# Gate and up products of a transformer feed-forward stage in token-major blocks, with transposes into the down product

## Chip, core and metric

One core of a Trainium2 chip runs the whole program. The metric is the device time of one execution in microseconds (us), the median of several runs. TensorE does the matrix products, VectorE (DVE) and ScalarE (ACT) the elementwise work, GpSimd (POOL) a few reductions, SyncE (SP) issues the weight transfers.

## What is computed

Three transformer layers in a row on 256 tokens of 1024 channels, all in float32: two layers of a first kind and one of a second. Each ends in the same feed-forward stage, the part that the change touches:

```python
h = rms_norm(x, g_pre_ffn[l])
f = (jax.nn.silu(h @ w_gate[l]) * (h @ w_up[l])) @ w_down[l]    # 1024 -> 2816 -> 1024
x = x + rms_norm(f, g_post_ffn[l])
```

Ahead of it stand, by layer, attention with a short convolution and gates (the first two) or stick-breaking attention with a pooling mixer (the third); the third also takes scales and shifts from a small conditioning product (`w_cond_2`).

## The kernel before

**Exact products from rounded operands.** Every weight and every activation is split in two float32r parts: H, a rounded copy made on ACT (`nc.scalar.copy`, L267 for weights), and L, the remainder made on DVE (`tensor_sub`, L268). A product is three matmuls: H·H, H·L and L·H. So each weight tile of 1 MB (`raw`, [128, 2048]) costs two copies on ACT and two subtractions on DVE, one for each half.

**The weight stream.** All weights are packed on the host in the order of use (`ORDER`, from `stream_order` and `ffn_order`), one 1 MB transfer for each entry, issued on SP's queue. `get(key)` hands out the next entry and first issues transfers five entries ahead (`LOOK_RAW`, four `raw` buffers) and splits three entries ahead (`LOOK`). Halves of split weights live in nine buffers (`NSPLIT`). Entries named `cond` belong to the conditioning product: they aren't split, two DVE operations (L490) consume each. Nine of them lie in the feed-forward stage of layer 0 and nine in that of layer 1.

**Two forms of product.** `mmB` is channel-major: the weights are the stationary operand and the 256 tokens the moving one. One entry gives 256 output channels as [128 channels, 2 x 256 tokens] in one PSUM bank with 48 matmuls of 256 columns. `mmA4` is token-major: 128 tokens of the activation are stationary, 512 columns of weights move. Two entries (`h` = 0, 1) give 512 channels, for one token tile `t` at a time, with 24 matmuls of 512 columns into one PSUM bank; both token tiles take 48. The down product `mmD2` moves 512 columns of `w_down` and has the activation, channel-major, as stationary operand: 24 matmuls for an entry over two token tiles and two column halves.

**The feed-forward stage** (`ffn`, L496). The first 512 of the 2816 channels are token-major ("block A"): for each token tile gate (`pgA`), silu into `sA`, up (`puA`), `tensor_mul` on DVE (L520). Since down wants channels on the partitions, a task `ptf` then does four TensorE transposes (L505), the H copy (L508) and the L subtraction (L509) into `fA`. The other 2304 channels are nine channel-major blocks of 256 (`pg`, silu, `pu`, the DVE product L536, the split into `fHL` L539 and L540), already in the form that down wants. One down entry follows each of these blocks from the second on. The last four down entries form a tail (`row_out`), which goes token tile by token tile so that the norm behind it can begin.

**Order of the work.** The program is written out by hand with a planner: `pe(ns)` advances a clock by the planned TensorE time, `spawn(gen, delay)` books a task, and `tick()` between parts of products emits the tasks that have come due; `drain()` emits all that is left. A scheduler then fixes the order on each engine from priorities and its own timing, and may take a ready instruction ahead of one that it believes not ready. On the chip each engine works its list in order. Three pools matter here: eight PSUM banks (four of them the down accumulators `dn`), 17 large (`s4`) and seven small (`s2`) activation buffers.

Of the kernel before, what the change touches and what calls it, by code (L numbers as in the profile page):

```python
# [24 lines left out]
NKV = 4  # L25
HD = 64
DFF = 2816
NFB = (DFF - 512) // 256
NDOWN = DFF // 256
TAIL = 4  # L30
EPS = 1e-6
# [24 lines left out]


def ffn_order(l, cond):
    o = [("gA", l, 0), ("gA", l, 1), ("uA", l, 0), ("uA", l, 1)]
    nd = 0  # L60
    for i in range(NFB):
        o += [("g", l, i), ("u", l, i)]
        if i >= 1:
            o.append(("d", l, nd))
            nd += 1
        if cond:
            o.append(cond.pop(0))
    while nd < NDOWN:
        o.append(("d", l, nd))
        nd += 1  # L70
    assert not cond
    return o


# [42 lines left out]
def pack_weights(inp):  # L117
    splits = dict(q=0, kv=1024, cb=1536, cc=2560, cx=3584, ga=4608, gb=5632)
    out = np.empty((len(ORDER), P, CH), np.float32)

    def put(i, w, r0, nk, c0, nc_):
        src = w[r0:r0 + nk * P, c0:c0 + nc_]
        if nk == 4:
            out[i].reshape(P, nk, nc_)[...] = src.reshape(nk, P, nc_).transpose(1, 0, 2)
        else:
            out[i].reshape(P, 2, nk, nc_ // 2)[...] = src.reshape(nk, P, 2, nc_ // 2).transpose(1, 2, 0, 3)

    for i, k in enumerate(ORDER):
        n = k[0]
        if n == "q":  # L130
            put(i, inp["w_in"][k[1]], 512 * k[3], 4, 512 * k[2], 512)
        elif n == "kv":
            put(i, inp["w_in"][k[1]], 512 * k[2], 4, 1024, 512)
        elif n in ("cc", "cx", "cb", "ga", "gb"):
            put(i, inp["w_in"][k[1]], 0, 8, splits[n] + 256 * k[2], 256)
        elif n == "cp":
            put(i, inp["w_conv_proj"][k[1]], 0, 8, 256 * k[2], 256)
        elif n == "ap":
            put(i, inp["w_attn_proj"][k[1]], 0, 8, 256 * k[2], 256)
        elif n == "cond":  # L140
            put(i, inp["w_cond_2"][0], 256 * k[2], 2, 1024 * k[1], 1024)
        elif n in ("q2", "k2", "v2", "u2"):
            put(i, inp["w_in_2"][0], 512 * k[1], 4, 512 * ("q2", "k2", "v2", "u2").index(n), 512)
        else:
            l = k[1]
            sfx, li = ("", l) if l < 2 else ("_2", 0)
            if n == "wo":
                put(i, inp["w_out" + sfx][li], 256 * k[2], 2, 0, 1024)
            elif n == "d":
                put(i, inp["w_down" + sfx][li], 256 * k[2], 2, 0, 1024)  # L150
            elif n in ("gA", "uA"):
                w = inp[("w_gate" if n == "gA" else "w_up") + sfx][li]
                put(i, w, 512 * k[2], 4, 0, 512)
            else:
                w = inp[("w_gate" if n == "g" else "w_up") + sfx][li]
                put(i, w, 0, 8, 512 + 256 * k[2], 256)
    return out


# [1 line left out]
def tile_model(ctx: ExitStack, tc: tile.TileContext, x_in, wpack, sink, convw, gains, c_in,  # L161
# [9 lines left out]
    def s4(name, shape=(P, D), dt=F32):  # L171
        return ac.tile(list(shape), dt, tag="s4", name=name, bufs=NS4)
# [4 lines left out]
    def ps1(name, shape=(P, 512), dt=F32):  # L177
        return pp.tile(list(shape), dt, tag="B", name=name, bufs=8)
# [2 lines left out]
        return sm.tile([P, n], dt, tag="sm", name=name, bufs=24)  # L181

    class Pair:
        """A [128, 8, 256] operand as float32r pairs, in two tiles of four k-tiles each."""

        def __init__(self, name):
            self.name = name
# [15 lines left out]
            nc.scalar.copy(h, src)  # L203
            nc.vector.tensor_sub(self.ks(1, k0, n)[:, :, ts_], src, h.bitcast(F32))

# [1 line left out]
    clock = [0.0]  # L207
    tasks = []

# [27 lines left out]
    def mm(o, a, b, start, stop, **kw):  # L237
        nc.tensor.matmul(o, a, b, start=start, stop=stop, **kw)  # L238

# [1 line left out]
    state = dict(raw=0, spl=0, use=0)  # L241
    raws, HL = {}, {}

# [37 lines left out]
        state["use"] += 1  # L281
        return HL.pop(i)

# [1 line left out]
    HC = [slice(0, 512), slice(512, 1024)]  # L285
    xt = [cst.tile([P, D], F32, tag=f"x{t}", name=f"x{t}") for t in range(2)]

# [35 lines left out]
        nc.sync.dma_start(csb, c_in)  # L323
        nc.sync.dma_start(pscale, pool_scale)

# [1 line left out]
    def hp():  # L327
        return nullcontext() if state["use"] == 0 else tc.high_priority(offset=PRIO)

# [12 lines left out]
        return rs  # L342

    class Norm:
        """rms norm of a token tile: vec() the vector part, tr() the transposes into xp."""

        def __init__(self, t, G, S, xp, name):
            self.t, self.G, self.S, self.xp, self.name = t, G, S, xp, name
# [19 lines left out]
        def tr(self):  # L368
            ts_ = slice(self.t * P, (self.t + 1) * P)
            for j in range(2):  # L370
                pt = ps1(f"pt_{self.name}{j}", (P, 4, P))
                for k in range(4):
                    nc.tensor.transpose(pt[:, k, :], self.h[:, (4 * j + k) * P:(4 * j + k + 1) * P], ident)
                    pe(107)
                with hp():
                    self.xp.put(4 * j, 4, pt, ts_)
                if j == 0:
                    yield TR_GAP
            yield None

    class Post:
        """x += rms(acc) * G, half by half as the accumulator's banks complete."""

        def __init__(self, t, acc, G, name):
            self.t, self.acc, self.G, self.name = t, acc, G, name
# [16 lines left out]
                    if after is not None:  # L402
                        after(c)

# [1 line left out]
    def mmB(ps, w, xp):  # L406
        for c in range(2):
            o = ps[:, c * T:(c + 1) * T]
# [41 lines left out]
        tick()  # L450

    def row_out(chunks, accs, started, make_post, after):
        """chunks: [(w, fh, fl)]; per token tile, half by half, then the norms."""
        n = len(chunks)
        for t in range(2):
            post = make_post(t, accs[t])
            for c in range(2):
                for i, (w, fh, fl) in enumerate(chunks):
                    mmD2(accs[t], w, fh, fl, t, c, not started and i == 0, i == n - 1)
                post.half(c)  # L460
            after(t, post)
# [32 lines left out]
            nc.scalar.dma_start(modd[r:r + 1, :], mrow[0:1, :])  # L494

    def ffn(l, xp, norms, make_post, after):  # L496
        order = [k for k in ORDER if k[0] in ("g", "u", "d") and k[1] == l]
        gw = [get(("gA", l, h)) for h in range(2)]
        uw = [get(("uA", l, h)) for h in range(2)]
        fA = [s4(f"fA{j}{l}", (P, 4, T), F32R) for j in range(2)]  # L500

        def ptf(t, s):
            pt = ps1(f"ptf{l}{t}", (P, 4, P))
            for k in range(4):
                nc.tensor.transpose(pt[:, k, :], s[:, k * P:(k + 1) * P], ident)  # L505
                pe(107)
            dst = (slice(None), slice(None), slice(t * P, (t + 1) * P))
            nc.scalar.copy(fA[0][dst], pt)  # L508
            nc.vector.tensor_sub(fA[1][dst], pt, fA[0][dst].bitcast(F32))  # L509
            yield None  # L510

        for t in range(2):
            finish(norms[t].gen)
            pg = ps1(f"pgA{l}{t}")
            mmA4(pg, gw, xp, t)
            s = s2(f"sA{l}{t}")
            nc.scalar.activation(s, pg, AF.Silu)
            pu = ps1(f"puA{l}{t}")
            mmA4(pu, uw, xp, t)
            nc.vector.tensor_mul(s, pu, s)  # L520
            spawn(ptf(t, s), 2.0)
        fs = [(fA[0][:, 0:2], fA[1][:, 0:2]), (fA[0][:, 2:4], fA[1][:, 2:4])]
        tail = []
        accs = []
        for key in order:
            cond_due()
            if key[0] == "g":
                pg = ps1(f"pg{l}{key[2]}")
                mmB(pg, get(key), xp)
                s = s2(f"s{l}{key[2]}")  # L530
                last = nc.scalar.activation(s, pg, AF.Silu)
            elif key[0] == "u":
                pu = ps1(f"pu{l}{key[2]}")
                mmB(pu, get(key), xp)
                f = s2(f"f{l}{key[2]}")
                nc.vector.tensor_mul(f, pu, s)  # L536
                fHL = s4(f"fHL{l}{key[2]}", (P, 2, 2, T), F32R)
                fv = f.rearrange("p (k t) -> p k t", k=2)
                nc.scalar.copy(fHL[:, 0], fv)  # L539
                nc.vector.tensor_sub(fHL[:, 1], fv, fHL[:, 0].bitcast(F32))  # L540
                fs.append((fHL[:, 0], fHL[:, 1]))
            else:
                j = key[2]
                if not accs:
                    drain()
                    accs = [[ps1(f"dn{l}_{t}{c}") for c in range(2)] for t in range(2)]
                if j < NDOWN - TAIL:
                    w = get(key)
                    for t in range(2):
                        for c in range(2):  # L550
                            mmD2(accs[t], w, fs[j][0], fs[j][1], t, c, j == 0, False)
                else:
                    tail.append((get(key), fs[j][0], fs[j][1]))
        if l == DEPTH - 1:
            with tc.issue_after(last.ins):
                nc.scalar.preload_act_table_set("natural_log_exp_and_others")
        row_out(tail, accs, True, make_post, after)

# [1 line left out]
    def attention(l, q, kf, v, op):  # L560
        kTh = s4(f"kTh{l}", (P, NKV, T), F32R)
        kTl = s4(f"kTl{l}", (P, NKV, T), F32R)
# [177 lines left out]
            mp.put(2 * j, 2, a)  # L740
        return mp

# [1 line left out]
    def stick(hp, qT, kT, v2, mp, psz, pend):  # L744
        ws = [None, None]

# [102 lines left out]
                pass  # L849
        return mp  # L850

# [1 line left out]
    xp = Pair("x0")  # L853
    norms = [Norm(t, G0, None, xp, f"n0{t}") for t in range(2)]
    norms[0].vec()
# [164 lines left out]
```

## Time and profile before

| | |
|---|---|
| device time, 3 runs | 1199.77 us median (1198.21 to 1200.64) |
| span of the profiled execution | 1197.6 us |
| mean granted TensorE clock | 0.993 |
| TensorE matmul busy | 1164.8 us (97%) |
| DVE, ACT busy | 774.7 us (65%), 617.2 us (52%) |
| moved by DMA | 235.60 MB, mean 197 GB/s |

The profile covers one execution and gives its span from the first instruction to the last; it shows no time for what lies outside, so that execution's whole time isn't known. The median of the runs stands 2.2 us above the span. Busy matmul time counts each matmul to its modelled end, and neighbours overlap: the pace of a product is read from the distance of starts, which the chain of work that ended last gives as a duration and a count. Starts and durations are in us, means of one instruction in ns.

### The profile page before, as it was taken

The numbers are of one execution on the slowest core, as the hardware profiler recorded it, in microseconds if no ns is written. First come the engines' busy times: TensorE is split into PE (matmuls) and PEld (weight loads), VectorE is DVE, ScalarE is ACT, GpSimd is POOL, SyncE is SP. The second block draws the span as 40 slices with busy tenths as digits, with TensorE's granted clock in tenths as the row PEclk, the third lists the DMA queues.
The fourth block names the chain that finished last, engine by engine and source line by source line (L and its number), as shares of the span: only waits on it lengthen the run. The fifth ranks groups of instructions, "written<-read, shape, count | busy, mean of one in ns | idle before, by whom it ended". The sixth has DMA issues, their size and how long they took to land.

```text
span 1197.6 us, 19239 instructions
## 1 busy us (share of the span) xinstructions
PE 1164.8 (97%) x7880; PEld 1066.8 (89%) x7880; DVE 774.7 (65%) x958; ACT 617.2 (52%) x927; POOL 129.1 (11%) x146
## 2 busy tenths in 40 slices
PE   6999999999999999999999999999999999999997
PEld 5899899988999987998999978999987777999996
DVE  6767645769676747677757568675858448654542
ACT  5766555546444436656545455444445545544441
POOL 1021300010202001022220012020201002000000
PEclk9999999999999999999999999999999999999999
DMA  8733344646676665633357546584866345644520
GB/s 319 269 141 111 129 149 176 250 173 252 229 259 245 221 236 182 241 106 141 141 176 281 192 160 246 213 309 173 325 216 218 135 159 176 246 175 177 204 79 36
DMA packets 36256, 235.60 MB, mean 197 GB/s; under 512 B 4668, under 2 KB 5180, under 8 KB 9416
## 3 DMA queue, kind: packets, MB, share of 16 engines
q1 hardware_dynamic: 33696, 225.41, 51.9%
q10 hardware_dynamic: 2472, 8.96, 2.3%
q8 instruction: 62, 1.02, 0.3%
q14 instruction: 26, 0.21, 0.1%
HBM read 233.28 MB, written 1.07 MB: 196 GB/s over the span
## 4 chain that ended last, share of the span: by engine, by line
PE 51%; POOL 2%; ACT 1%; DVE 1%; issue 1%; POOLq 0%; DVEq 0%; ACTq 0%
PE pu L238 10%; PE dn L238 9%; PE pg L238 8%; PE wo L238 2%; PE pcp L238 2%; PE pap L238 2%; PE pga L238 2%; PE pgb L238 2%; PE pcx L238 2%; PE pcb L238 1%; PE pgA L238 1%; PE puA L238 1%; PE z L238 1%; PE po L238 1%; PE pv L238 1%
## 5 line engine op out<-in xcount | busy, mean ns | idle before, releaser
L268 DVE TENSOR_TENSOR L<-raw,H 128x1024 fp32r<-128x1024 f32 x374 | 472.6, 1270 | 228.3 <-ACT H L267 215.6
L267 ACT CAST H<-raw 128x1024 fp32r<-128x1024 f32 x374 | 390.7, 1049 | 366.8 <-PE pu L238 72.8
L238 PE MATMUL dn<-H,fHL 128*128 128x512 f32 x432 | 116.3, 391 | 0.0
L238 PEld LDWEIGHTS dn<-H,fHL 128*128 128x128 f32 x432 | 79.8, 188 | 15.6
L635 POOL TENSOR_SCALAR P<-P,rd 128x256 f32<-128x256 f32 x64 | 48.1, 769 | 228.2 <-DVE rd L633 67.3
L238 PE MATMUL dn<-L,fHL 128*128 128x512 f32 x216 | 66.8, 390 | 0.0
L493 POOL PARTITION_ALL_REDUCE mrow<-cacc x6 | 40.1, 6676 | 219.5 <-DMA raw<-in_wpack_dram 180.8
L490 DVE SCALAR_TENSOR_TENSOR cacc<-raw,silu_c,cacc 128x1024 f32<-128x1024 f32 x48 | 61.4, 1279 | 0.4
L238 PEld LDWEIGHTS dn<-L,fHL 128*128 128x128 f32 x216 | 40.6, 188 | 8.5
L536 DVE TENSOR_TENSOR f<-pu,s 128x512 f32<-128x512 f32 x27 | 18.6, 690 | 30.4 <-PE pu L238 30.4
L238 PE MATMUL pg<-xf1H,H 128*128 128x256 f32 x144 | 35.4, 283 | 0.0
L238 PE MATMUL pg<-xf0H,H 128*128 128x256 f32 x144 | 35.3, 283 | 0.0
L238 PE MATMUL pg<-xf2H,H 128*128 128x256 f32 x144 | 35.3, 283 | 0.0
L238 PE MATMUL pu<-xf0H,H 128*128 128x256 f32 x144 | 35.3, 283 | 0.0
L238 PE MATMUL pu<-xf0L,H 128*128 128x256 f32 x144 | 35.3, 283 | 0.0
L238 PE MATMUL pu<-xf1H,H 128*128 128x256 f32 x144 | 35.3, 283 | 0.0
L238 PE MATMUL pu<-xf1L,H 128*128 128x256 f32 x144 | 35.3, 283 | 0.0
L238 PE MATMUL pu<-xf2H,H 128*128 128x256 f32 x144 | 35.3, 283 | 0.0
L238 PE MATMUL pu<-xf2L,H 128*128 128x256 f32 x144 | 35.3, 283 | 0.0
L238 PE MATMUL pg<-xf1L,H 128*128 128x256 f32 x144 | 35.3, 283 | 0.0
L238 PE MATMUL pg<-xf0L,H 128*128 128x256 f32 x144 | 35.3, 283 | 0.0
L238 PE MATMUL pg<-xf2L,H 128*128 128x256 f32 x144 | 35.3, 283 | 0.0
(400 smaller groups left out, 3057.0 us busy)
## 6 DMA issues: line engine op xcount, KB each, us to landing
raw<-in_wpack_dram SPq DMA_DIRECT2D x209, 1024.0 KB, 4.9
raw<-in_wpack_dram SPq DMA_DIRECT2D x4, 512.0 KB, 8.5
gpm<-in_gains_dram ACTq DMA_DIRECT2D x3, 512.0 KB, 3.7
gpf<-in_gains_dram ACTq DMA_DIRECT2D x3, 512.0 KB, 5.1
gqf<-in_gains_dram ACTq DMA_DIRECT2D x2, 512.0 KB
out_dram<-x SPq DMA_DIRECT2D x4, 256.0 KB, 3.8
pmat<-in_pmat_dram SPq DMA_DIRECT2D x2, 384.0 KB, 6.8
x<-in_x_dram SPq DMA_DIRECT2D x2, 256.0 KB, 2.7
```

The lines of the kernel that those rows point to most:

```text
L238: nc.tensor.matmul(o, a, b, start=start, stop=stop, **kw)
L267: nc.scalar.copy(H, rv)
L268: nc.vector.tensor_sub(L, rv, H.bitcast(F32))
L490: nc.vector.scalar_tensor_tensor(a3, w[:, k], silu_c[:, 2 * j + k:2 * j + k + 1], a3, ALU.mult, ALU.add)
L493: nc.gpsimd.partition_all_reduce(mrow, a, P, bass_isa.ReduceOp.add)
L536: nc.vector.tensor_mul(f, pu, s)
L635: nc.gpsimd.tensor_scalar(Pt[:, hh, :], Pt[:, hh, :], rd[:, hh:hh + 1], 0.0, ALU.mult, ALU.add)
```

## The change

Gate and up take 512 channels at a time in token-major form five times (2560 channels); the last 256 channels stay channel-major. In each later token-major block gate runs for both token tiles first, then up for both. Each block ends in two `ptf` tasks, ten for a layer. In `ORDER` two down entries follow a token-major block from the second on (one after the last), and the `cond` entries lie after a block's gate and after its up entries, what is left ahead of the last 256 channels. `drain()` stays ahead of the first down product, which now comes right behind the second block's up. Comments that the diff drops are left out here.

```diff
-NFB = (DFF - 512) // 256
+NFB = DFF // 512
+REST = DFF - 512 * NFB
...
 def ffn_order(l, cond):
-    o = [("gA", l, 0), ("gA", l, 1), ("uA", l, 0), ("uA", l, 1)]
+    o = [(n, l, 0, h) for n in ("gA", "uA") for h in range(2)]
     nd = 0
-    for i in range(NFB):
-        o += [("g", l, i), ("u", l, i)]
-        if i >= 1:
+    for b in range(1, NFB):
+        for n in ("gA", "uA"):
+            o += [(n, l, b, h) for h in range(2)] + cond[:1]
+            del cond[:1]
+        while nd < min(2 * b, NDOWN - TAIL):
             o.append(("d", l, nd))
             nd += 1
-        if cond:
-            o.append(cond.pop(0))
+    o += cond
+    cond.clear()
+    o += [("g", l), ("u", l)]
     while nd < NDOWN:
...
+        def gate(b, t, w):
+            pg = ps1(f"pgA{l}{b}{t}")
+            mmA4(pg, w, xp, t)
+            s = s2(f"sA{l}{b}{t}")
             nc.scalar.activation(s, pg, AF.Silu)
-            pu = ps1(f"puA{l}{t}")
-            mmA4(pu, uw, xp, t)
+            return s
+
+        def up(b, t, w, s, fA):
+            pu = ps1(f"puA{l}{b}{t}")
+            mmA4(pu, w, xp, t)
             nc.vector.tensor_mul(s, pu, s)
-            spawn(ptf(t, s), 2.0)
...
+            spawn(ptf(b, t, s, fA), 2.0)
...
+        for b in range(NFB):
+            fA = [s4(f"fA{j}{l}{b}", (P, 4, T), F32R) for j in range(2)]
+            gw = weights("gA", b)
+            if b == 0:
+                uw = weights("uA", b)
+                for t in range(2):
+                    finish(norms[t].gen)
+                    up(b, t, uw, gate(b, t, gw), fA)
+            else:
+                s = [gate(b, t, gw) for t in range(2)]
+                uw = weights("uA", b)
+                for t in range(2):
+                    up(b, t, uw, s[t], fA)
+            fs += [(fA[0][:, 0:2], fA[1][:, 0:2]), (fA[0][:, 2:4], fA[1][:, 2:4])]
+            down()
+        pg = ps1(f"pg{l}")
+        mmB(pg, get(("g", l)), xp)
...
+        pu = ps1(f"pu{l}")
+        mmB(pu, get(("u", l)), xp)
...
+        down()
+        tail = [(get(("d", l, j)), fs[j][0], fs[j][1]) for j in range(NDOWN - TAIL, NDOWN)]
```

`weights` gets the two entries of a product, after any `cond` entry that is due; `down` does the down entries that come next in `ORDER`, up to the tail.

## Rows read from the trace of the kernel before

**Rows 1.** The page's first part: busy time of each engine, its share of the span, instructions.

```profile
PE 1164.8 (97%) x7880; PEld 1066.8 (89%) x7880; DVE 774.7 (65%) x958; ACT 617.2 (52%) x927; POOL 129.1 (11%) x146
```

**Rows 2.** Busy time of each engine in the dense part of the three feed-forward stages, from the end of block A's transposes to the last up product (us of the window, then busy us of PE, weight load, DVE, ACT and POOL with instruction counts, granted clock, DMA share, GB/s).

```profile
292.50:436.00 143.50, 143.50 (x1042) 136.56 (x1041) 99.36 (x89) 63.32 (x70) 13.92 (x2) 1.00 0.68 250
740.50:880.00 139.50, 139.50 (x1013) 132.75 (x1012) 97.24 (x86) 62.62 (x68) 13.86 (x2) 1.00 0.70 253
1030.50:1175.00 144.50, 144.50 (x1034) 136.83 (x1033) 71.40 (x68) 61.02 (x67) 0.00 (x0) 1.00 0.44 158
```

**Rows 3.** What TensorE waited for over the whole span (total us, times, longest): the one row of the feed-forward stage's transposes.

```profile
PE ptf L505 <- DVE sA L520: 0.6, 1, 0.6
```

**Rows 4.** The chain of work that ended last, layer 1, from the end of block A on (start us, us, what, count).

```profile
739.45 0.61 DVE sA L520
740.06 0.04 issue
740.11 0.66 PE ptf L505 x4
740.76 2.87 PE pg L238 x24
743.64 5.76 PE pu L238 x48
749.40 5.76 PE pg L238 x48
755.16 5.76 PE pu L238 x48
760.92 5.47 PE dn L238 x24
```

**Rows 5.** The same chain, layer 2, block A and the first channel-major product.

```profile
1015.82 2.73 PE pgA L238 x12
1018.55 0.44 PE ptf L505 x4
1018.99 2.77 PE pgA L238 x12
1021.76 5.44 PE puA L238 x24
1027.20 2.88 PE pg L238 x24
1030.07 0.44 PE ptf L505 x4
1030.51 2.87 PE pg L238 x24
```

**Rows 6.** The instructions on the tile `ptf`: duration in ns (min/median/max), first and last start.

```profile
L505 PE MATMUL ptf<-ident,sA x24: 270/272/331, 283.9 to 1030.2; 128*128 128x128 f32 x24
L508 ACT CAST fA<-ptf x6: 578/584/591, 284.6 to 1030.5; 128x512 fp32r<-128x512 f32 x6
L509 DVE TENSOR_TENSOR fA<-ptf,fA x6: 676/682/689, 285.8 to 1031.4; 128x512 fp32r<-128x512 f32 x6
```

**Rows 7.** DVE's groups in the dense part of layer 1 (740.5 to 880 us): busy us, mean ns of one, idle time ahead of them and what ended it.

```profile
L268 DVE TENSOR_TENSOR L<-raw,H 128x1024 fp32r<-128x1024 f32 x50 | 66.6, 1339 | 32.9 <-ACT H L267 32.4
L490 DVE SCALAR_TENSOR_TENSOR cacc<-raw,silu_c,cacc 128x1024 f32<-128x1024 f32 x16 | 20.5, 1280 | 0.1
L536 DVE TENSOR_TENSOR f<-pu,s 128x512 f32<-128x512 f32 x9 | 6.2, 690 | 8.9 <-PE pu L238 8.9
L540 DVE TENSOR_TENSOR fHL<-f,fHL 128x512 fp32r<-128x512 f32 x8 | 5.5, 683 | 0.0
```

**Rows 8.** DVE in order of time around two channel-major blocks of layer 1 (start us, us, instruction; in brackets the idle time before and what ended it).

```profile
760.95 0.69 DVE L536 TENSOR_TENSOR f<-pu,s 128x512 f32<-128x512 f32 x1 [1.48 <-PE pu L238]
...
776.56 2.60 DVE L490 SCALAR_TENSOR_TENSOR cacc<-raw,silu_c,cacc 128x1024 f32<-128x1024 f32 x2
779.08 0.68 DVE L536 TENSOR_TENSOR f<-pu,s 128x512 f32<-128x512 f32 x1
```

**Rows 9.** Busy time of each engine in block A of layer 1, second half, and in one channel-major block of layer 1 (columns as in rows 2).

```profile
725.00:737.00 12.00, 12.00 (x59) 9.99 (x58) 11.50 (x9) 8.23 (x9) 6.13 (x1) 1.00 0.62 213
766.40:777.90 11.50, 11.50 (x97) 11.50 (x97) 10.14 (x10) 4.32 (x5) 0.00 (x0) 1.00 0.73 272
```

**Rows 10.** TensorE in order of time at the start of block A, layer 1.

```profile
713.17 0.48 PE L238 MATMUL pgA<-H,xf1H 128*128 128x512 f32 x1
713.48 0.40 PE L238 MATMUL puA<-H,xf1H 128*128 128x512 f32 x1
713.72 0.39 PE L238 MATMUL pgA<-H,xf1L 128*128 128x512 f32 x1
```

**Rows 11.** ACT in order of time in block A of layer 1, gate of the second token tile (idle time before, and what ended it).

```profile
726.24 1.06 ACT L267 CAST H<-raw 128x1024 fp32r<-128x1024 f32 x1 [3.08 <-PE pgA L238]
727.60 1.05 ACT L267 CAST H<-raw 128x1024 fp32r<-128x1024 f32 x1 [0.30 <-PE pgA L238]
...
729.43 1.05 ACT L267 CAST H<-raw 128x1024 fp32r<-128x1024 f32 x1 [0.30 <-PE pgA L238]
730.86 1.06 ACT L267 CAST H<-raw 128x1024 fp32r<-128x1024 f32 x1 [0.38 <-PE pgA L238]
```

More of the change, by code (lines that the diff above doesn't have):

```diff
@@ L70, in ffn_order @@
         nd += 1
-    assert not cond
     return o
@@ L152, in pack_weights @@
                 w = inp[("w_gate" if n == "gA" else "w_up") + sfx][li]
-                put(i, w, 512 * k[2], 4, 0, 512)
+                put(i, w, 512 * k[3], 4, 512 * k[2], 512)
             else:
                 w = inp[("w_gate" if n == "g" else "w_up") + sfx][li]
-                put(i, w, 0, 8, 512 + 256 * k[2], 256)
+                put(i, w, 0, 8, 512 * NFB, REST)
     return out
@@ L496, in ffn, with ptf @@
     def ffn(l, xp, norms, make_post, after):
[L497 to L503, printed above, removed]
+        fs = []
+        accs = []
+        def ptf(b, t, s, fA):
+            pt = ps1(f"ptf{l}{b}{t}", (P, 4, P))
             for k in range(4):
@@ L510, in ptf, with weights @@
             yield None
[L512 to L516, printed above, removed]
+        def weights(n, b):
+            w = []
+            for h in range(2):
+                cond_due()
+                w.append(get((n, l, b, h)))
+            return w
+        def gate(b, t, w):
+            pg = ps1(f"pgA{l}{b}{t}")
+            mmA4(pg, w, xp, t)
+            s = s2(f"sA{l}{b}{t}")
             nc.scalar.activation(s, pg, AF.Silu)
-            pu = ps1(f"puA{l}{t}")
-            mmA4(pu, uw, xp, t)
+            return s
@@ L520, in ffn @@
+        def up(b, t, w, s, fA):
+            pu = ps1(f"puA{l}{b}{t}")
+            mmA4(pu, w, xp, t)
             nc.vector.tensor_mul(s, pu, s)
-            spawn(ptf(t, s), 2.0)
[L522 to L525, printed above, removed]
-            cond_due()
[L527 to L543, printed above, removed]
+            spawn(ptf(b, t, s, fA), 2.0)
@@ L544, in ffn, with down @@
+        def down():
+            cond_due()
+            while state["use"] < len(ORDER) and ORDER[state["use"]][:2] == ("d", l):
+                j = ORDER[state["use"]][2]
+                if j >= NDOWN - TAIL:
+                    return
                 if not accs:
                     drain()
[L546 to L553, printed above, removed]
+                    accs.extend([ps1(f"dn{l}_{t}{c}") for c in range(2)] for t in range(2))
+                w = get(("d", l, j))
+                for t in range(2):
+                    for c in range(2):
+                        mmD2(accs[t], w, fs[j][0], fs[j][1], t, c, j == 0, False)
+                cond_due()
@@ new lines, in ffn @@
+        for b in range(NFB):
[9 more added lines that the diff above has]
+                uw = weights("uA", b)
+                for t in range(2):
+                    up(b, t, uw, s[t], fA)
+            fs += [(fA[0][:, 0:2], fA[1][:, 0:2]), (fA[0][:, 2:4], fA[1][:, 2:4])]
+            down()
@@ new lines, in ffn @@
+        pg = ps1(f"pg{l}")
+        mmB(pg, get(("g", l)), xp)
+        s = s2(f"s{l}")
+        last = nc.scalar.activation(s, pg, AF.Silu)
+        pu = ps1(f"pu{l}")
+        mmB(pu, get(("u", l)), xp)
+        f = s2(f"f{l}")
+        nc.vector.tensor_mul(f, pu, s)
+        fHL = s4(f"fHL{l}", (P, 2, 2, T), F32R)
+        fv = f.rearrange("p (k t) -> p k t", k=2)
+        nc.scalar.copy(fHL[:, 0], fv)
+        nc.vector.tensor_sub(fHL[:, 1], fv, fHL[:, 0].bitcast(F32))
+        fs.append((fHL[:, 0], fHL[:, 1]))
```

## The prediction

> **What bounds the kernel now.** I read first the busy shares: TensorE 97%, the weight load beside it, DVE 65%, ACT 52% [rows 1]. A share over the span says little about one stage, so next the windows of the three feed-forward stages. From the end of block A to the last up product TensorE is busy for all of 143.5, 139.5 and 144.5 us at a granted clock of 1.00, while DVE works 99, 97 and 71 us in them and DMA stays at 0.44 to 0.70 of its time [rows 2]. TensorE alone sets the pace here: a change in these stages is worth what it changes in TensorE's issue time, plus any new wait of TensorE. The third view is the list of TensorE's waits. Of the six `ptf` groups of the whole program only one waited, for 0.6 us [rows 3]. The fourth is the chain, which gives the pace of each form of product [rows 4, 5]; busy time can't, because neighbouring matmuls overlap in it.
>
> **Gate and up.** A channel-major product of 256 channels holds 48 matmuls and takes 5.76 us, row after row [rows 4]: 0.120 us for each. If time went by columns alone, 512 columns would take twice that, 0.240 us, and the change would gain nothing. But 24 token-major matmuls of 512 columns take 5.44 us, 0.227 us for each [rows 5]. So the same arithmetic, 512 channels for 256 tokens, costs 2 x 5.76 = 11.52 us in the old form and 2 x 5.44 = 10.88 us in the new. The instructions are half as many and each has a fixed part: 2 x 0.120 - 0.227 = 0.013 us.
>
> Eight of the nine channel-major blocks of a layer become four token-major ones. Removed: 16 products x 5.76 = 92.16 us. Added: 16 half products x 5.44 = 87.04 us. Gain 5.12 us a layer, 15.4 us in three. As other bound I take the slowest row of 24 such matmuls, the down product's 5.47 us [rows 4]: 87.52 us, gain 4.64 a layer, 13.9 us in all.
>
> **The transposes.** Each new token-major block adds two `ptf` groups: eight more in a layer, 24 in all, four transposes each. In the chain a group between token-major matmuls takes 0.44 us, and the twelve matmuls behind it 2.77 us instead of 2.73 [rows 5]: 0.48 us. Inside a channel-major product it is 0.44 with nothing behind it (2.88 before, 2.87 after) [rows 5]. All new groups but some at a block's end lie between matmuls of 512 columns, so I take 0.48: 24 x 0.48 = 11.5 us; lower bound 24 x 0.44 = 10.6 us.
>
> The chain's 0.44 us is far below four times one transpose's own duration of 272 ns [rows 6], so they overlap like other matmuls. The Trainium skill speaks against the change here: "TensorE: Matmul & The Clock Gate", Part 4 (PE-mode transpose), gives about 275 ns for a transpose in a kernel and says that SBUF access latency dominates it. The trace agrees on the duration, 272 ns, but not on what it costs in a row: four take 0.44 us and not 1.09. If the durations did add up, 24 groups would cost 26.1 us and the change would lose; that is the third rival.
>
> **Other engines.** Work on DVE and ACT stays the same in number: 512 columns of silu, of gate times up, of copy and of subtraction for each 256 channels. Only the source moves from SBUF to PSUM: the subtraction takes 682 ns where `fHL`'s takes 683 [rows 6, 7]. The weights are the same 1 MB entries in equal number, 33 and nine `cond` ones in layers 0 and 1, on the same queue; the last `cond` entry moves ahead of the last 256 channels. I cost this at nothing; TensorE's work covers it, with DVE idle for 42 of 139.5 us [rows 2].
>
> **Weight buffers.** A gate over token tile 0 frees none of its four half buffers; they come free one by one over token tile 1. In block A of layer 1 the splits indeed wait for `pgA` and follow each other 1.4 us apart [rows 11]. With nine buffers, four gate and four up halves are held at once. I walked through a block of 33 us: the second to fourth half of the next gate can be split while up runs over token tile 1, when the halves of this up come free at 1.4 us steps. Their first use is two down entries (2 x 5.47 us) later; the L work of four halves is 4 x 1.34 = 5.4 us [rows 7]. So nothing is late, and I cost it at nothing. If the two down entries weren't between, a part of these 5.4 us would show.
>
> **Waits of the transposes.** Here the change adds risk. The transposes wait for DVE's `tensor_mul` (0.69 us), and TensorE's list stops behind them. The planner books them 2.0 us after the up product, and parts of products are 1.3 us, so they come two parts, 12 matmuls or 2.73 us [rows 5], into the next product. DVE begins the multiplication 0.03 us after the product's end where it sat waiting [rows 4, 8], and 1.18 us late behind a `cond` operation (up product due to end at 777.90, on the rhythm of 5.76 and 5.47 us from rows 4) [rows 4, 8]. Then it is done 1.9 us after the product's end and 0.06 us later the transposes can go [rows 4]: 0.8 us to spare. In the dense part I expect no wait. The one that there was (0.6 us) stood behind block A of layer 1, with DVE busy 11.5 of 12 us against 10.1 of 11.5 later [rows 9]; block A keeps its place.
>
> One place has no such margin. `drain()` now emits the last transposes of the second block right behind its up product. In the written order TensorE would stand for 0.03 + 0.69 + 0.06 = 0.78 us, and with one DVE operation of 1.28 us in front for 2.06 us; three times, 2.3 to 6.2 us. It can be nothing too: the scheduler fills gaps that it foresees, as when it put the first matmul of `puA` between the first two of `pgA` [rows 10], and here the down product's matmuls stand ready. I take 0.3 us a layer, nearer to nothing because this wait hangs on a single DVE operation: 0.9 us.
>
> **The sum.** -15.4 + 11.5 + 0.9 = -3.0 us. The profiled span would be 1194.6 instead of 1197.6 us, and the median, which stands 2.2 us above that span, 1199.8 - 3.0 = 1196.8 us. A measurement of this kernel can't tell changes under 0.2% (2.4 us) from none, so the forecast lies not far beyond that line. Bounds without a rival: best -15.4 + 10.6 = -4.8, 1195.0 us; worst of the pace terms -13.9 + 11.5 = -2.4.
>
> **Rivals.**
> 1. *The drained transposes wait in full.* Speaks for it that TensorE's list did stop for `ptf` once [rows 3], against it rows 10. Then -3.9 + 2.3 to 6.2: -1.6 to +2.3 us, 1198.2 to 1202.1 us, no difference to be told.
> 2. *Slower: transposes wait for DVE throughout.* Place: the multiplication queued on DVE behind L subtractions, which now come in bursts of four when up frees its buffers. Price: 0.6 us for each of the 24 new groups, as at 740.11 [rows 3, 4]: -3.9 + 14.4 = +10.5, 1210.3 us. It decides from (3.9 + 2.4) / 24 = 0.26 us a group on. For it: DVE is busy 70% of the dense part in layers 0 and 1 [rows 2]. Against it: DVE idles 1.48 us ahead of the multiplication at 760.95 and is late at 779.08 by one operation only [rows 8], and layer 2 has no `cond` work.
> 3. *Transposes in a row don't overlap*, which the page's 275 ns would suggest: 24 x 4 x 0.272 = 26.1 us, so -15.4 + 26.1 = +10.7, 1210.5 us. Rows 5 contradict it twice.
>
> **Chances.** Forecast 0.54. First rival 0.27, second 0.11, third 0.02; the remaining 0.06 is for a change of order on the engines that I don't see, either way. Most of the forecast's 0.54 lies beyond 0.2%, but its own bounds touch the line, and some of the 0.06 is faster: faster 0.52, same 0.33, slower 0.15. The range reaches from the best pace, with half a microsecond for layers' ends, 1194.5, into the first rival, 1201 us; it leaves out rival 2 and 3 and the far end of rival 1.
>
> **What would show it.** In the profile after: TensorE instructions 7880 - 1152 + 96 = 6824; the chain with dozens of `pgA` and `puA` matmuls at 2.72 us, each `ptf` group at 0.44 us; no wait of `ptf` above 0.3 us on average; a dense stage some 1.0 to 1.6 us shorter in each layer. Wrong would be: a `ptf` row among TensorE's waits with many entries (rival 2) or three of 0.8 us and more (rival 1); a wait of `pgA` or `puA` for H or L (the buffers); a product of 24 that takes more than 5.5 us in the new blocks; or TensorE idle at a layer's end, where nothing should have moved.

## The result: slower, and the profile after

| | before | changed |
|---|---|---|
| device time, 7 runs each | 1199.77 us median (1198.21 to 1201.22) | 1203.97 us median (1201.25 to 1206.68) |
| span of the profiled execution | 1197.6 us | 1200.3 us |
| mean granted clock of the profiled execution | 0.993 | 0.993 |

The ratio is 1.0035, with a 95% interval of 1.0023 to 1.0046: slower by 4.2 us, where 3.0 us less were forecast. The profiled execution shows 2.7 us of it.

Part 1 of the page after, against [rows 1]:

```profile
PE 1161.0 (97%) x6824; PEld 1014.9 (85%) x6824; DVE 778.7 (65%) x958; ACT 616.5 (51%) x927; POOL 126.6 (11%) x146
```

TensorE has the 6824 instructions of the forecast, DVE and ACT their old counts. The list of TensorE's waits over the span, the row that answers to [rows 3] (total us, times, longest):

```profile
PE ptf L506 <- DVE sA L530: 6.7, 5, 2.6
```

0.6 us in one wait has become 6.7 us in five, three of them in layer 1. The chain there, against [rows 4]:

```profile
748.11 7.72 PE puA L241 x34
...
760.44 0.66 PE ptf L506 x4
761.10 10.93 PE dn L241 x48
772.02 10.88 PE pgA L241 x48
782.90 8.17 PE puA L241 x36
791.07 0.44 PE ptf L506 x4
791.51 1.41 PE puA L241 x6
...
799.60 0.63 PE ptf L506 x4
800.23 8.20 PE dn L241 x36
```

Gate over both token tiles takes 10.88 us for 48 matmuls and a group of transposes between matmuls 0.44 us, as in [rows 5]. But two groups of transposes stand behind a stretch in which the chain leaves TensorE. TensorE's own rows at these places and at the third (idle time in brackets):

```profile
758.87 0.61 PE L241 MATMUL puA<-L,xf1H 128*128 128x512 f32 x2
760.44 0.66 PE L506 MATMUL ptf<-ident,sA 128*128 128x128 f32 x4 [0.96 <-DVE sA L530]
760.86 0.47 PE L241 MATMUL dn<-H,fA 128*128 128x512 f32 x1
...
799.60 0.63 PE L506 MATMUL ptf<-ident,sA 128*128 128x128 f32 x4 [2.62 <-DVE sA L530]
...
862.05 0.52 PE L506 MATMUL ptf<-ident,sA 128*128 128x128 f32 x3 [0.98 <-DVE sA L530]
```

The first is the drained place, and it has its like in layer 0 (0.96 us at 316.80) and layer 2 (1.18 us at 1053.85): no down matmul stands ahead of the transposes in TensorE's list. The other two lie in the dense part, where no wait was expected. In the chain a group behind a wait also takes about 0.65 instead of 0.44 us, so a wait costs 0.2 us more than its length.

How long each feed-forward stage takes, read from TensorE's starts (first `pgA` matmul to the first down matmul of the tail, us), for all kernels of this study, which the next section describes:

| | layer 0 | layer 1 | layer 2 | sum |
|---|---|---|---|---|
| before | 165.6 | 166.4 | 166.0 | 498.1 |
| changed | 165.4 | 169.4 | 166.1 | 500.9 |
| changed, second profile | 165.4 | 171.0 | 166.1 | 502.5 |
| no drain | 164.9 | 169.7 | 164.6 | 499.2 |
| later transposes | 165.1 | 165.2 | 165.5 | 495.9 |
| no drain, later transposes | 164.2 | 165.4 | 164.6 | 494.3 |
| the same, still later | 164.2 | 164.2 | 164.6 | 493.1 |
| no drain, later, no reductions | 164.2 | 164.2 | 164.8 | 493.2 |
| no drain, later, no transposes in blocks 1 to 4 | 160.4 | 160.4 | 160.8 | 481.7 |
| no drain, later, conditioning moved | 164.5 | 165.2 | 164.6 | 494.2 |
| changed, no reductions | 165.5 | 165.5 | 166.0 | 497.0 |
| before, no reductions | 165.6 | 165.7 | 166.0 | 497.3 |

The 2.8 us between the first two sums are the 2.7 us of the spans: the whole loss of the profiled execution lies in these stages.

### The profile page after: what moved, and what is told of

Same layout as the page of the kernel before. It is cut to its first block, busy times and chain, and to the rows that moved or that the text cites. A ratio compares the mean times of both kernels' runs of the same rounds, so it can differ in the third digit from the quotient of the medians.

```text
span 1200.3 us, 17134 instructions
## 1 busy us (share of the span) xinstructions
PE 1161.0 (97%) x6824; PEld 1014.9 (85%) x6824; DVE 778.7 (65%) x958; ACT 616.5 (51%) x927; POOL 126.6 (11%) x146
## 4 chain that ended last, share of the span: by engine, by line
PE 50%; POOL 2%; DVE 2%; ACT 1%; issue 1%; POOLq 0%; DVEq 0%; ACTq 0%
PE dn L241 9%; PE pgA L241 9%; PE puA L241 8%; PE wo L241 2%; PE pu L241 2%; PE pcp L241 2%; PE pap L241 2%; PE pga L241 2%; PE pgb L241 2%; PE pcx L241 2%; PE pcb L241 1%; PE z L241 1%; PE po L241 1%; PE pv L241 1%; PE pg L241 1%
## 5 line engine op out<-in xcount | busy, mean ns | idle before, releaser
L241 PE MATMUL dn<-H,fA 128*128 128x512 f32 x480 | 130.1, 392 | 0.0
L241 PEld LDWEIGHTS dn<-H,fA 128*128 128x128 f32 x480 | 88.9, 188 | 17.6
L241 PE MATMUL dn<-L,fA 128*128 128x512 f32 x240 | 74.3, 390 | 0.0
L241 PEld LDWEIGHTS dn<-L,fA 128*128 128x128 f32 x240 | 45.1, 188 | 9.5
L241 PE MATMUL puA<-H,xf1H 128*128 128x512 f32 x80 | 31.7, 397 | 0.0
L241 PE MATMUL puA<-H,xf0H 128*128 128x512 f32 x80 | 31.7, 397 | 0.0
L241 PE MATMUL puA<-H,xf2H 128*128 128x512 f32 x80 | 31.6, 395 | 0.0
L241 PE MATMUL pgA<-H,xf0H 128*128 128x512 f32 x80 | 31.4, 393 | 0.0
L241 PE MATMUL pgA<-H,xf1H 128*128 128x512 f32 x80 | 31.4, 393 | 0.0
L241 PE MATMUL pgA<-H,xf2H 128*128 128x512 f32 x80 | 31.3, 392 | 0.0
```

## Experiments

All edits are to the changed kernel unless said otherwise; the times of before are those of runs on the same chip.

**Without the drain.**

```diff
                 if not accs:
-                    drain()
+                    pass
                     accs.extend([ps1(f"dn{l}_{t}{c}") for c in range(2)] for t in range(2))
```

> The changed kernel without the drain ahead of the first down product, so the second block's last transposes come 12 matmuls into the down product as in the later blocks. In the changed kernel's profile (span 1200.3 us) the transposes waited 3.1 us at the three drained places and 3.6 us at two other places of layer 1. Theory (the loss is made of these waits, and they are of two kinds): the three drained waits go, the two others stay, span about 1197.2 us. Rival (the waits only show that DVE is late, and the time comes back as a wait for split weights): the wait moves to pgA, puA or dn and the span stays at 1199.5 us or more.

1197.31 us median of ten executions (1197.15 without one of 6.5 ms, which the ratio leaves out) against 1199.52, ratio 0.9979 (0.9968 to 0.9990), span 1197.2 us. The transposes at the three drained places come 12 matmuls into the down product and wait no more. What is left of `ptf` waits is 3.9 us in three: 2.3 and 1.1 us at the same two places of layer 1, and a new one of 0.4 us in layer 0. The expectation held.

**Later transposes.** The tasks come 24 matmuls behind the up product instead of 12; the drain stays.

```diff
-            spawn(ptf(b, t, s, fA), 2.0)
+            spawn(ptf(b, t, s, fA), 4.5)
```

> The changed kernel with the transposes booked 4.5 us after their up product instead of 2.0, the drain kept: they come 24 matmuls later instead of 12. Theory: the two waits of layer 1 behind DVE's queue (2.6 and 1.0 us) go, the drained ones (3.1 us) stay, span about 1196.7 us. Rival (weights too late in layer 1): the 3.6 us stay as a wait for H or L, span 1200 us.

1196.09 us, ratio 0.9964 (0.9951 to 0.9976), span 1194.7 us. The waits of layer 1's dense part are gone; three are left, each at a drain, of 0.75 us: the 0.78 us that the prediction had worked out for a drained group with DVE free. The expectation had kept them at their 0.96 to 1.18 us. In the changed kernel the subtraction on the block's first `ptf` and another DVE operation (at 758.09 and 758.93 us in layer 1) stand ahead of the multiplication; with the later booking they come behind it.

**Both.**

> Both edits at once. Theory: TensorE waits for no transposes in the feed-forward stages, span 1200.3 - 6.7 = 1193.6 us, which is the 3.8 us below the kernel before that pace and transposes were to give; median about 1196 us. Rival 1 (the pace gain or the transposes were mis-sized): no waits, but a span above 1195.5 us. Rival 2 (DVE or the weight stream sets the pace): new waits, span above 1197 us.

1193.76 us, ratio 0.9949 (0.9931 to 0.9967). The stages take 494.3 us, 3.8 less than before, as the pace and the transposes were to give. One wait of 1.0 us is left in layer 1, at 793 us, where none was expected. (The span of 1189.1 us also has less half clock in the attention stages, so the stages are the better measure.)

**What the transposes cost.** With both edits, but in blocks 1 to 4 the copies read `sA` as it stands:

```diff
+            if b > 0:
+                dst = (slice(None), slice(None), slice(t * P, (t + 1) * P))
+                sv = s.rearrange("p (k c) -> p k c", k=4)
+                nc.scalar.copy(fA[0][dst], sv)
+                nc.vector.tensor_sub(fA[1][dst], sv, fA[0][dst].bitcast(F32))
+                yield None
+                return
             pt = ps1(f"ptf{l}{b}{t}", (P, 4, P))
```

> As the run with both edits, but the later token-major blocks leave their TensorE transposes out: the copies to fA read sA as it stands, so that the down product multiplies wrong channels. It measures what 24 groups of transposes cost on TensorE. Theory: 24 x 0.48 us, 11.5 us less than with both edits, span about 1182 us. Rival (transposes cost their own durations, 24 x 1.09 us): 26 us less. Rival (they cost more than their issue, by what they delay): 14 us or more.

1181.23 us; the stages fall from 494.3 to 481.7 us. Of these 12.6 us 1.0 was the wait that is left with the transposes, so 24 groups cost 11.6 us, 0.48 us each. Four transposes in a row don't cost four times their 272 ns [rows 6]; the third rival is out.

**The changed kernel again.**

> The changed kernel unaltered, for a second profile and more times on the chip of the other runs. Its first profile is 2.7 us above the profile of the kernel before, its median 4.2 us. Theory: the difference of 1.5 us is the granted clock, which falls for 3.4 us behind a long wait of TensorE in some executions; so a run with a mean clock of 0.991 is about 2 us longer than the one at 0.993, and its profile shows half clock at 785 to 805 us, behind the wait of 2.6 us. Rival: the slower runs show more waits, or half clock in the attention stages only, as in the kernel before.

1203.80 us median (1201.79 to 1205.45), ratio 1.0036 (1.0023 to 1.0049): the loss repeats. The second profile has a span of 1201.8 us and the same five waits, 6.7 us in all, so more waits don't explain what it takes longer. TensorE's clock does. Busy times, clock and DMA around the longest wait (columns as in [rows 2]), first in the second profile, then in the first:

```profile
795.00:798.50 3.50, 1.78 (x8) 1.13 (x6) 3.50 (x4) 0.00 (x0) 1.28 (x1) 1.00 0.49 133
798.50:806.00 7.50, 6.61 (x25) 5.55 (x26) 4.81 (x6) 2.69 (x3) 0.00 (x0) 0.77 0.69 236
```

```profile
794.50:798.50 4.00, 2.48 (x11) 1.71 (x10) 4.00 (x4) 0.40 (x1) 1.98 (x1) 1.00 0.34 92
798.50:806.00 7.50, 6.40 (x31) 5.38 (x32) 5.23 (x6) 2.69 (x3) 0.00 (x0) 1.00 0.80 283
```

In both TensorE idles 2.62 us. In the second profile the granted clock behind it averages 0.77: a part of the stretch at 1.2 GHz, the rest at 2.4 GHz, and 25 matmuls started in it instead of 31. Layer 1's stage takes 171.0 instead of 169.4 us, 1.6 us more. The profile without the drain has it too, 0.83 behind its wait of 2.3 us; in the kernel before the feed-forward stages ran at 1.00 [rows 2]. So a wait of this length costs its length and, in some executions, 1.6 us of slow clock. This is how 2.7 us of one execution become 4.2 us of the medians, as far as two profiles can tell; which of the other executions had it can't be seen.

**What made DVE late.** DVE in order of time behind the first up product of layer 1's third token-major block (block A is the first; the expectation below calls it the second), changed kernel, first profile; then POOL in the same stretch:

```profile
788.38 0.69 DVE L530 TENSOR_TENSOR sA<-puA,sA 128x512 f32<-128x512 f32 x1 [1.27 <-PE puA L241]
788.99 1.28 DVE L493 SCALAR_TENSOR_TENSOR cacc<-raw,silu_c,cacc 128x1024 f32<-128x1024 f32 x1
790.38 6.74 DVE L271 TENSOR_TENSOR L<-raw,H 128x1024 fp32r<-128x1024 f32 x2
797.04 0.68 DVE L510 TENSOR_TENSOR fA<-ptf,fA 128x512 fp32r<-128x512 f32 x1
797.64 1.21 DVE L271 TENSOR_TENSOR L<-raw,H 128x1024 fp32r<-128x1024 f32 x1
798.78 0.68 DVE L530 TENSOR_TENSOR sA<-puA,sA 128x512 f32<-128x512 f32 x1
```

```profile
790.37 6.12 POOL L496 PARTITION_ALL_REDUCE mrow<-cacc  x1 [57.66 <-DVE cacc L493]
```

Two subtractions take 6.74 us instead of 2.4 (the first 5.61, the second 1.21), just while POOL reduces the conditioning sums over the partitions. The multiplication that the transposes need stands behind them and starts at 798.78, though its up product ended near 794.3. The wait at 862.05 has the same picture ahead of it (DVE, then POOL):

```profile
854.89 6.41 DVE L271 TENSOR_TENSOR L<-raw,H 128x1024 fp32r<-128x1024 f32 x2 [0.20 <-ACT H L270]
861.22 0.68 DVE L530 TENSOR_TENSOR sA<-puA,sA 128x512 f32<-128x512 f32 x1
```

```profile
853.46 7.21 POOL L496 PARTITION_ALL_REDUCE mrow<-cacc  x1 [56.97 <-DVE cacc L493]
```

This run takes the reductions away:

```diff
             mrow = s4(f"mrow{r}")
-            nc.gpsimd.partition_all_reduce(mrow, a, P, bass_isa.ReduceOp.add)
-            nc.scalar.dma_start(modd[r:r + 1, :], mrow[0:1, :])
+            nc.scalar.dma_start(modd[r:r + 1, :], a[0:1, :])
```

> The changed kernel without the six reductions over partitions on POOL (L496): one row of the partial sums goes to DRAM instead of the total, which leaves the conditioning values wrong. The transfers and DVE's own work stay. In the profile of the changed kernel a subtraction of weights on DVE took 5.6 us instead of 1.2 while such a reduction ran at 790 us, and the multiplication of the second block stood behind it. Theory: the two waits of layer 1 (2.6 and 1.0 us) go, the three behind the drain stay (3.1 us), span about 1196.7 us. Rival (the burst of subtractions and the conditioning work alone make DVE late): the two waits stay, span 1199.5 us or more.

1197.91 us, ratio to before 0.9990 (0.9980 to 0.9999), span 1194.6 us. The `ptf` waits fall from 6.7 us in five to 3.1 in three, all at drains; layer 1's stage from 169.4 to 165.5 us. (The span falls 2.1 us below the expected one; 0.3 us of it lie in the stages, and in layer 0's attention the granted clock is 1.00 from 76 to 84 us, where the changed kernel has 0.79.) The same place of DVE's list now:

```profile
787.04 1.27 DVE L493 SCALAR_TENSOR_TENSOR cacc<-raw,silu_c,cacc 128x1024 f32<-128x1024 f32 x1
788.43 2.58 DVE L271 TENSOR_TENSOR L<-raw,H 128x1024 fp32r<-128x1024 f32 x2
790.92 0.68 DVE L508 TENSOR_TENSOR fA<-ptf,fA 128x512 fp32r<-128x512 f32 x1
792.37 0.69 DVE L528 TENSOR_TENSOR sA<-puA,sA 128x512 f32<-128x512 f32 x1 [0.76 <-PE puA L241]
```

The same two subtractions take 2.58 us, and DVE is there before the product ends. The burst of subtractions alone makes nothing late.

**The reductions in the kernel before.** The same edit on the kernel before:

> The kernel before without the six reductions on POOL (wrong conditioning values). In its profile the reductions stretch subtractions on DVE to 4.7 us too, but of its six groups of transposes only one waited, 0.6 us. Theory (the channel-major form is covered against a late DVE): 0.6 us less in layer 1's stage, 165.8 us instead of 166.4, and within 0.2% of the kernel before. Rival (the reductions cost the kernel before as much as the changed one, and so explain none of the difference): 3 us less or more.

1199.27 us against 1199.47, ratio 0.9996 (0.9987 to 1.0005): no difference. Layer 1's stage loses 0.8 us, and no `ptf` wait is left: the one of [rows 3] had been the work of a reduction, too. The reductions stretch DVE's subtractions in the kernel before, too:

```profile
794.91 0.69 DVE L536 TENSOR_TENSOR f<-pu,s 128x512 f32<-128x512 f32 x1 [0.72 <-PE pu L238]
795.52 4.15 DVE L268 TENSOR_TENSOR L<-raw,H 128x1024 fp32r<-128x1024 f32 x1
799.59 0.68 DVE L540 TENSOR_TENSOR fHL<-f,fHL 128x512 fp32r<-128x512 f32 x1
```

Here the delay falls on `fHL`, for which no TensorE instruction had to wait. The token-major form put TensorE's transposes 2.7 us behind their up product, and the DVE multiplication between the two can stand behind a subtraction that is held up by as much as 4.4 us.

**Conditioning entries elsewhere.** With both edits, layer 1's nine entries and their reductions moved out of its feed-forward stage:

```diff
-N_COND = {("ap", 0): 2, ("ffn", 0): 9, ("gb", 1): 2, ("ga", 1): 2, ("ffn", 1): 9}
+N_COND = {("ap", 0): 4, ("ffn", 0): 8, ("gb", 1): 4, ("ga", 1): 4, ("ap", 1): 4}
```

> No drain, transposes booked 4.5 us later, and the nine conditioning entries of layer 1's feed-forward stage moved into the mixers and the stage of layer 0, their reductions with them. The run without that move kept one wait of 1.0 us at 793 us, behind a reduction. Theory: that wait goes, the stage of layer 1 takes 164.3 us instead of 165.4, median 1 us below 1193.8. Rival: the reductions hold up DVE in the mixers of layer 1, where TensorE then waits, and the median rises to 1195 us or more.

1204.01 us, ratio 1.0039 (1.0024 to 1.0054): the rival was right. No `ptf` wait is left in the stage, but the first `pgA` matmul of layer 1 starts at 720.85 us instead of 707.43 with both edits alone. DVE is busy 63.8 of 70 us from 640 to 710 us there, and TensorE waits in `wo`:

```profile
PE wo L241 <- DVE L L271: 4.4, 2, 3.5
```

The longer of the two ends with a subtraction that took 5.25 us from 696.42 on, during a reduction. There is half clock behind it, too: the granted clock averages 0.76 from 699 to 706 us. How the 13 us divide among waits, clock and other delays wasn't followed further. The stage itself takes 165.2 us instead of the expected 164.3; 0.7 us of that is a wait of `pgA` for its input `xf1L` at the start.

**Still later transposes.** No drain and a delay of 6.0 instead of 4.5 us, 30 matmuls behind the up product:

```diff
-            spawn(ptf(b, t, s, fA), 2.0)
+            spawn(ptf(b, t, s, fA), 6.0)
```

> No drain, and the transposes 6.0 us after their up product: another six matmuls or 1.4 us later than with 4.5, nothing else changed. Theory: the last wait of the variant with 4.5 us (1.0 us, behind a reduction at 785 us) goes, every feed-forward stage takes 164.2 to 164.8 us, and the median is 0.5 to 1.5 us under that variant's 1193.8, some 0.5% under the kernel before. Rival (DVE falls behind without bound in layer 1): the wait stays, the median too.

1192.92 us (1190.32 to 1193.31) against 1199.47, ratio 0.9936 (0.9923 to 0.9949): the fastest version that leaves nothing out, with no `ptf` wait left. The intervals don't tell its median from that of both edits; the stages do, 493.1 against 494.3 us. They are as short as without any reduction (493.2): all the reductions' delay is absorbed. With no drain, a delay of 4.5 us and no reductions, expected as follows, the median was 1192.11 us:

> No drain, transposes 4.5 us after their product, and no reductions on POOL (wrong conditioning values). Theory: no wait of TensorE for transposes is left, each of the three feed-forward stages takes 164.2 to 164.7 us from its first matmul to the tail, against 165.6, 166.4 and 166.0 in the kernel before. Rival (something else delays layer 1): its stage still takes over 165 us.

No `ptf` wait is left. Two of its stages take 164.2 us and the third 164.8, 0.1 us above the expected range.

## Why the prediction was wrong

- **What bounds the kernel, the pace, the transposes: right.** TensorE sets the pace. Without waits the stages take 493.1 us in the new form and 497.3 us in the old (before, no reductions): 4.2 us less, where 15.4 - 11.5 = 3.9 us were summed. The transposes measured 0.48 us a group, the figure taken.
- **Other engines, weight buffers: right in what they say, but POOL was left out.** Neither `pgA` nor `puA` waits for H or L, nor does the burst of subtractions make DVE late.
- **The drained transposes: mis-sized, and for a wrong reason.** 0.3 us a layer was taken; it was 0.96, 0.96 and 1.18 us, 3.1 us in all and 0.2 us more behind each. The step that failed is "the scheduler fills gaps that it foresees": it put nothing there. [rows 10] show that it can; they don't show that it will. The first rival, with 2.3 to 6.2 us, had it. Why the list was left so isn't known.
- **"In the dense part I expect no wait": wrong.** 2.6 and 1.0 us, shown to be the work of the reductions on POOL (gone without them, absorbed by later transposes). The step behind it took DVE's worst delay from one row [rows 8], one `cond` operation of 1.28 us. The rows had the larger delay: in [rows 7] a subtraction takes 1339 ns on average, above the 1.2 us of one that nothing holds up; POOL is busy 14 us in that window [rows 2]; and in [rows 9] POOL works 6.1 of the 12 us ahead of the one wait, which the prediction laid to a busy DVE. Rival 2 had the right place, TensorE behind DVE's list, but a wrong cause (bursts) and a wrong count (two groups, not 24).
- **The clock: not in the sum.** In a stage that had run at 1.00 a long wait of TensorE had half clock behind it in two of the three profiles with such a wait (after 2.6 and 2.3 us), 1.6 us more in the one that can be compared.

The stages' balance for the profiled execution: -4.2 us of issue, +6.7 us of waits where the wait-free form has none, about +1.0 us for five slower groups behind them, and -0.8 us since the old form is compared with its own delay by a reduction: +2.7 us, against 2.8 measured. The medians' further 1.4 us fit the slow clock, which the executions without a profile don't show.

## What to carry to other kernels

A saving of a fraction of a percent in the bound engine's issue holds only while every instruction that it waits for has margin: list, for each new dependency on another engine, the longest stretch for which that engine was ever held up (the maximum, not the mean), and book the dependent work later than that. Here a booking of 6.0 instead of 2.0 us, at no cost, and one `drain()` less turned 0.35% slower into 0.64% faster. An engine with 11% busy time can be the cause: look at what a long instruction does to the others while it runs.

## What the runs showed of the hardware

- **A reduction on POOL holds up some DVE operations and not others.** While it ran, subtractions of `raw` and H, both in SBUF, took up to 5.6 instead of 1.2 us (the largest of the changed kernel; 4.7 before), but the product of `pu` in PSUM and `s` took its usual 0.69 us at 794.91. In each of the six reductions of the changed kernel one subtraction was held, and it ended 0.5 us before the reduction did, whether it had begun early (5.6 us long) or late (2.6 us long); so the hold can be nearly as long as the reduction, 6.1 us. A subtraction that began together with the reduction at 853.46 took its usual 1.23 us. The Trainium skill has this rule in "SBUF — State Buffer", section "Who interferes with whom": a DVE instruction with two SBUF inputs contends with a GpSimd instruction that reads SBUF, one with at most one SBUF input, outside the modes that use two ports, doesn't. The trace agrees in both halves, but for the subtraction at 853.46.
- **Half clock behind a wait.** With the same wait of 2.62 us the granted clock stayed at 1.00 in one profile and averaged 0.77 over the following 7.5 us in another.
- **Half clock elsewhere.** The mean granted clock of the executions varied between 0.990 and 0.998, mostly by half clock in the attention stages, which the change doesn't touch. The fastest version had 0.995 to 0.998, the kernel before beside it 0.991 to 0.996; so of its 6.6 us only 5.0 are in the feed-forward stages. The other 1.6 us are what one stretch of half clock cost in layer 1, and its profile has one less: 1.00 from 519 to 527 us, where the kernel before has 0.79. Why it has one less stays open.
